# A decoder layer on one core: the norm's factor applied after the products, first up products of block one alone, and the last split moved forward

## The chip, the cores and the metric

The kernel runs on one core of one Trainium2 chip. The metric is the device time of one execution in microseconds (us); it is given as a median of several runs. One of the executions is recorded by the hardware profiler, and all rows of the trace are from that execution. TensorE is called PE, its weight load PEld, VectorE DVE, ScalarE ACT, GpSimd POOL, SyncE (which issues most of the loads) SP.

## The reference

One decoder layer on 256 tokens with 2048 channels, in float32. `rmsnorm(x, g)` is `x * rsqrt(mean(x * x) + 1e-6) * g`.

```
h = rmsnorm(x, norm_mix_pre)
xr, yr, q, k, v, g_rnn, g_attn = split(h @ w_in)
y_rnn = rg_lru(conv(xr)) * gelu(yr)
y_att = attention(rope(q), rope(k), v)          # 32 heads, 4 key heads, window 128, sinks
mix = sigmoid(g_rnn) * (y_rnn @ w_rnn_proj) + sigmoid(g_attn) * (y_att @ w_attn_proj)
x = x + rmsnorm(mix @ w_out, norm_mix_post)
h = rmsnorm(x, norm_mlp_pre)
x = x + rmsnorm(square(relu(h @ w_mlp_up)) @ w_mlp_down, norm_mlp_post)
```

## The kernel before

**Data and weights.** The 256 tokens are two blocks of 128 (`tb` 0 and 1, "block one" and "block two"). Weights come as 128x2048 chunks; class `Stream` (L52) loads each as two half chunks of 128x1024 (512 KB) on SP's queue, in one fixed order, as far ahead as its buffers allow. To keep float32 accuracy with the faster fp32r products, every operand is cut in two parts: `two_parts` (L89) casts the half chunk to `whi` on ACT (L92) and subtracts to get `wlo` on DVE (L93). A product of activations a and weights w is the sum of three matmuls: a high by w high, a low by w high, a high by w low. `split_to`, `ahead` and `half` (L78, L120, L124) make the parts ahead of their use; `split_sums` (L96) does the same for the chunks of the down product that go through a seven-product scheme (`SEVEN`).

**Front.** x is normed before it is transposed: four squares a block (two on ACT L354, two on DVE L358), the norm factor (`rms`, L330), then a multiply by factor and gain (`scale`, L363), where the gain has been spread over the partitions by PE (`gain_b`, L348). `turn` transposes four 128x128 tiles into one bank of PSUM, and `part` cuts them into the high part (ACT, L375) and the low part (DVE, L376) of hT. The first product, keys and values (`kv`), runs between: hi products L390 and L391, lo products L388. For a stretch of this stage the low parts of the weights are made on POOL (`ws.low`, L409). All is pinned in the order written (`keep_in_program_order`). Seven dummy matmuls (L342) stand ahead.

**What follows.** Attention gates and queries by key head group (`b_pass512`, L263), the attention, the recurrent branch (`a_pair`, L225, gives two row blocks of xr or yr; `conv`, `gelu`), the gated merge, and the output product o in two halves of 1024 columns (`b_pass1024`, L854).

**Middle.** `finish` (L888) runs at high priority after each block of o: squares on ACT (L893), multiply by the gains on DVE (L894), `rms`, four multiply-adds L907 that make h2, and `transpose_split` (L277) of four quarters, each one bank with ACT's high part (L285) and DVE's low part (L286) of h2T. Behind block two's norm stand six dummies (L903). Then the up product runs in pairs: `a_pair` takes both blocks at once (hi: 128x512 with the high and the low part of both blocks, L235; lo: 128x256, L238), eight of each in a half chunk. The residual sum (L945, L946) is fed in piece by piece by `pump`.

**Tail.** `down` (L995) is called for each half of the hidden channels and of the columns. In its last call, `early` (L1091) adds the stored first half to four sums on DVE, and `finish` (L1103) takes the four results in turn: DVE adds (L1108), ACT squares (L1112), DVE multiplies by the gain (L1113, L1118), `rms`, four multiply-adds (L1124), and the stores. Instructions of different parts are ordered by a scheduler that follows priorities (`high_priority`), explicit "issue after" edges and pinned sequences.

## Time and profile before

| | us |
|---|---|
| median of 3 runs (lowest, highest) | 1553.24 (1552.12, 1554.74) |
| the profiled execution | 1548.21 |
| its span | 1546.4 |
| PE busy | 1516.1 |
| DVE busy | 1098.4 |
| ACT busy | 824.0 |
| POOL busy | 12.1 |
| mean HBM rate (GB/s) | 192 |

Times in rows of the trace count from the start of the span. A row of the timeline gives start, busy time, engine, line, operation, output and inputs, shape and count; in brackets stands how long the engine was idle ahead of it and what ended that. A row of a group gives busy time in all, mean ns of one, and idle time before it. A matmul's row shows 0.39 us for 128x512, but matmuls are pipelined: the distance from one start to the next is what a matmul costs.

### The profile page before, as it was taken

Reading aid. Unit: us, or ns where it says so; the run is one execution under the profiler, and the core shown is the slowest. Engines: PE = TensorE matmul, PEld = TensorE weight load, DVE = VectorE, ACT = ScalarE, POOL = GpSimd, SP = SyncE. Lnnn points to the kernel's source line nnn. Section 1 sums busy time; section 2 is a strip of 40 time slices with the busy share of each in tenths; the row PEclk is TensorE's granted clock in tenths of the full one; section 3 lists DMA queues with packets and bytes.
Section 4 is the critical chain, followed back from the end, with each engine's and each line's share of the span. In section 5 each row is a group of like instructions: output and inputs, shape, how many; then the busy total and the mean of one; then the engine's idle time right before and its main releaser. Section 6 shows DMA issues by size and latency. Waiting matters only on the chain.

```text
span 1546.4 us, 19944 instructions
## 1 busy us (share of the span) xinstructions
PE 1516.1 (98%) x7562; PEld 1264.5 (82%) x7562; DVE 1098.4 (71%) x1338; ACT 824.0 (53%) x1116; POOL 12.1 (1%) x14
## 2 busy tenths in 40 slices
PE   7999999999999999999999999999999999999996
PEld 5887777788888888888877888888888888888885
DVE  5666666856759867546666876688886766678897
ACT  4545555646647757444354655555454555555552
POOL 3000000000000000000000000000000000000000
PEclk9999999999999999999999999999999999999999
DMA  6454354354655575665663865556667655576663
GB/s 247 161 179 146 127 174 155 125 185 156 227 193 175 166 222 177 203 196 184 243 237 108 271 202 185 190 182 210 215 205 234 204 188 190 181 282 193 202 212 129
DMA packets 82322, 296.19 MB, mean 192 GB/s; under 512 B 9521, under 2 KB 9777, under 8 KB 81201
## 3 DMA queue, kind: packets, MB, share of 16 engines
q1 hardware_dynamic: 78768, 285.48, 56.6%
q10 hardware_dynamic: 3458, 9.45, 1.6%
q8 instruction: 59, 0.97, 0.2%
q14 instruction: 37, 0.30, 0.1%
HBM read 288.60 MB, written 6.29 MB: 191 GB/s over the span
## 4 chain that ended last, share of the span: by engine, by line
PE 81%; DVE 8%; DMA 5%; ACT 3%; issue 2%; DVEq 0%; POOL 0%; ACTq 0%; SPq 0%; POOLq 0%
PE ps L235 21%; PE ps L238 10%; PE dQ L987 5%; DMA wraw<-in_w_dn 4%; DVE wlo L93 4%; PE dP L987 2%; PE s L987 2%; PE gr L253 2%; PE pa L253 2%; PE pr L257 2%; PE pr L255 2%; PE gr L255 2%; PE q L253 2%; PE pr L253 2%; PE gr L257 2%
## 5 line engine op out<-in xcount | busy, mean ns | idle before, releaser
L93 DVE TENSOR_TENSOR wlo<-wraw,whi 128x1024 fp32r<-128x1024 f32 x524 | 635.3, 1222 | 317.5 <-ACT whi L92 316.4
L92 ACT CAST whi<-wraw 128x1024 fp32r<-128x1024 f32 x528 | 549.3, 1050 | 582.5 <-PE ps L235 140.2
L235 PE MATMUL ps<-h2T,whi 128*128 128x512 f32 x1024 | 256.6, 392 | 0.6 <-DVE h2T L286 0.6
L235 PEld LDWEIGHTS ps<-h2T,whi 128*128 128x128 f32 x1024 | 184.2, 189 | 33.8 <-DVE h2T L286 0.8
L238 PEld LDWEIGHTS ps<-h2T,wlo 128*128 128x128 f32 x1024 | 139.7, 190 | 10.0
L238 PE MATMUL ps<-h2T,wlo 128*128 128x256 f32 x1024 | 142.8, 282 | 0.0
L235 PE MATMUL ps<-hT,whi 128*128 128x512 f32 x512 | 130.2, 394 | 0.0
L987 PE MATMUL dQ<-whi,uT 128*128 128x512 f32 x288 | 106.9, 390 | 0.0
L235 PEld LDWEIGHTS ps<-hT,whi 128*128 128x128 f32 x512 | 91.7, 189 | 18.0 <-issue 1.8
L238 PEld LDWEIGHTS ps<-hT,wlo 128*128 128x128 f32 x512 | 70.0, 190 | 5.0
L238 PE MATMUL ps<-hT,wlo 128*128 128x256 f32 x512 | 71.9, 283 | 0.0
L987 PEld LDWEIGHTS dQ<-whi,uT 128*128 128x128 f32 x288 | 54.2, 188 | 11.3 <-ACT whi L92 0.3
L987 PE MATMUL dQ<-wlo,uT 128*128 128x512 f32 x144 | 56.5, 393 | 4.6 <-DVE wlo L93 4.6
L987 PE MATMUL dCs<-whi,uT 128*128 128x512 f32 x144 | 54.5, 395 | 0.0
L112 DVE TENSOR_TENSOR tlo<-t,thi 128x1536 fp32r<-128x1536 f32 x28 | 49.2, 1756 | 7.3 <-ACT thi L111 7.1
L987 PE MATMUL dP<-whi,uT 128*128 128x512 f32 x144 | 53.8, 389 | 0.0
L253 PE MATMUL ga<-whi,hT 128*128 128x512 f32 x128 | 51.2, 400 | 0.0
L253 PE MATMUL q<-whi,hT 128*128 128x512 f32 x128 | 51.1, 399 | 0.0
L257 PE MATMUL ga<-whi,hT 128*128 128x512 f32 x128 | 50.3, 393 | 0.0
L255 PE MATMUL ga<-wlo,hT 128*128 128x512 f32 x128 | 50.3, 393 | 0.0
L255 PE MATMUL q<-wlo,hT 128*128 128x512 f32 x128 | 50.2, 392 | 0.0
L253 PE MATMUL gr<-whi,hT 128*128 128x512 f32 x128 | 50.0, 391 | 0.0
(272 smaller groups left out, 2581.3 us busy)
## 6 DMA issues: line engine op xcount, KB each, us to landing
wraw<-in_w_up SPq DMA_DIRECT2D x128, 512.0 KB, 4.6
wraw<-in_w_dn SPq DMA_DIRECT2D x128, 512.0 KB, 4.6
wraw<-in_w_g SPq DMA_DIRECT2D x64, 512.0 KB, 4.7
wraw<-in_w_xy SPq DMA_DIRECT2D x64, 512.0 KB, 4.5
wraw<-in_w_q SPq DMA_DIRECT2D x32, 512.0 KB, 4.2
wraw<-in_w_ap SPq DMA_DIRECT2D x32, 512.0 KB, 3.8
wraw<-in_w_rp SPq DMA_DIRECT2D x32, 512.0 KB, 4.4
wraw<-in_w_out SPq DMA_DIRECT2D x32, 512.0 KB, 5.0
```

Of the source, the lines that this page charges most:

```text
L92: self.pin(self.nc.scalar.copy(hi, src))
L93: self.pin(self.low.tensor_tensor(lo, src, hi.bitcast(F32), ALU.subtract))
L112: v.tensor_tensor(lo, t, hi.bitcast(F32), ALU.subtract)
L235: mm(both, hi[:, k * P : k * P + P], a.rearrange("p a b -> p (a b)"), start=half == 0 and k == 0, stop=False)
L238: mm(ps[:, f, 1, :], lo[:, k * P : k * P + P], a[:, 0, :], start=False, stop=half == 1 and k == 7)
L253: mm(banks[tb][n], a[:, 0, t], hi[:, n * 512 : n * 512 + 512], start=first, stop=False)
L255: mm(banks[tb][n], a[:, 0, t], lo[:, n * 512 : n * 512 + 512], start=False, stop=False)
L257: mm(banks[tb][n], a[:, 1, t], hi[:, n * 512 : n * 512 + 512], start=False, stop=last)
L987: mm(b, a[x], w[y], start=not begun and i == 0, stop=tail and i == 2)
```

## The change

Four things are joined.

**Front.** x is transposed as it comes. The gain is no longer spread by PE; it is loaded as a 128x16 column table (`gcol`, on ACT's queue) and applied by the copy that takes a tile out of PSUM, tile by tile: `quad` has four 128x128 copies with a scale on ACT, and four multiply-subtracts on DVE; `both` the same with two 128x256. The norm factor r0 comes later: it goes into the rope tables, into the copy of v, into the scale of the tanh of both gates (`rhalf`), and, spread over the partitions by two matmuls (`spread_r`), into a multiply on DVE after each pair of xr and yr (`r_all`, 16 in all). The squares stand behind the kv product. The loads of x and of the first weights alternate by halves. POOL makes no low parts any more.

PE at the start of the program, before (x is the input block, kv the two sums):

```order
L342 MATMUL warm<-ones 128x128 x7
L348 MATMUL gain_b<-gain,ones 128x512 x4
L369 MATMUL ptr<-ident,x_76 128x128 x8
L390 MATMUL kv_141<-whi_169,hT_137 128x512
L391 MATMUL kv_141<-whi_169,hT_137 128x512
L390 MATMUL kv_141<-whi_169,hT_137 128x512
L391 MATMUL kv_141<-whi_169,hT_137 128x512
L369 MATMUL ptr<-ident,x_76 128x128 x4
L390 MATMUL kv_141<-whi_175,hT_137 128x512
L391 MATMUL kv_141<-whi_175,hT_137 128x512
L390 MATMUL kv_141<-whi_175,hT_137 128x512
```

and after the change (front is a PSUM bank that takes four transposed tiles, hT their two parts):

```order
L366 MATMUL warm<-ones 128x128 x7
L387 MATMUL front<-ident,x_76 128x128 x8
L366 MATMUL warm<-ones 128x128 x4
L429 MATMUL kv_126<-whi_153,hT_120 128x512 x4
L387 MATMUL front<-ident,x_77 128x128 x8
L436 MATMUL kv_126<-wlo_155,hT_120 128x512 x2
L429 MATMUL kv_127<-whi_153,hT_120 128x512 x4
L429 MATMUL kv_126<-whi_189,hT_120 128x512 x4
L436 MATMUL kv_127<-wlo_155,hT_120 128x512 x2
L436 MATMUL kv_126<-wlo_191,hT_120 128x512 x2
L429 MATMUL kv_127<-whi_189,hT_120 128x512 x4
```

Gone are the four gain products between the dummies and the first transposes; four more dummies stand behind the first eight transposes, and block two's first transposes come behind four kv products, where they came behind twelve and all of block one's transposes.

**Middle.** The dummies of block two's norm go. The high parts of the first six half chunks of up are made during the end of o (`high_to`; four of them in two spare rooms, `uphi`), together with two whole splits. Their hi products are cut by block: `ahead_of` runs those of block one right behind o, while block two's norm goes on, then block two's, with block two's transposes at fixed places between; the low products of both blocks follow, six half chunks in a row. Two of o's banks are copied to SBUF on ACT so that they come free.

DVE at the end of o, before (h_6164 is block one, h_6165 block two; h2T_6174 to 6177 are the four quarters of the MLP's input):

```order
L907 SCALAR_TENSOR_TENSOR h_6164<-h_6164,st,xg_6162 128x512 x4
L286 TENSOR_TENSOR h2T_6174<-ptr,h2T_6174 128x4x128
L894 TENSOR_TENSOR h_6165<-o_6503,gpg_6157 128x512
L286 TENSOR_TENSOR h2T_6175<-ptr,h2T_6175 128x4x128
L286 TENSOR_TENSOR h2T_6176<-ptr,h2T_6176 128x4x128
L894 TENSOR_TENSOR h_6165<-o_6504,gpg_6157 128x512
L334 TENSOR_REDUCE st<-sqs 128x1
L336 RECIPROCAL st<-st 128x1
L907 SCALAR_TENSOR_TENSOR h_6165<-h_6165,st,xg_6163 128x512 x2
L286 TENSOR_TENSOR h2T_6177<-ptr,h2T_6177 128x4x128
L907 SCALAR_TENSOR_TENSOR h_6165<-h_6165,st,xg_6163 128x512 x2
L286 TENSOR_TENSOR h2T_6174<-ptr,h2T_6174 128x4x128
```

and after the change (h_6211 is block one, h_6212 block two, h2T_6221 to 6224 the quarters):

```order
L951 SCALAR_TENSOR_TENSOR h_6211<-h_6211,st,xg_6209 128x512 x4
L305 TENSOR_TENSOR h2T_6221<-ptr,h2T_6221 128x4x128
L943 TENSOR_TENSOR h_6212<-o_6550,gpg_6204 128x512
L305 TENSOR_TENSOR h2T_6222<-ptr,h2T_6222 128x4x128
L943 TENSOR_TENSOR h_6212<-o_6551,gpg_6204 128x512
L356 TENSOR_REDUCE st<-sqs 128x1
L305 TENSOR_TENSOR h2T_6223<-ptr,h2T_6223 128x4x128
L358 RECIPROCAL st<-st 128x1
L951 SCALAR_TENSOR_TENSOR h_6212<-h_6212,st,xg_6210 128x512 x4
L305 TENSOR_TENSOR h2T_6224<-ptr,h2T_6224 128x4x128
L305 TENSOR_TENSOR h2T_6221<-ptr,h2T_6221 128x4x128
L305 TENSOR_TENSOR h2T_6222<-ptr,h2T_6222 128x4x128
```

The last low part of block one (h2T_6224, before h2T_6177) stood between block two's multiply-adds, and now stands behind all four; the first part of block two follows it at once.

**Tail.** In the last call of `down` the last half chunk is split as soon as the last of the seven-product chunks is through; the sums of `early` and the gain multiplies on the stored half are told to issue behind that split.

DVE in the tail before (wlo_12544 and wlo_12548 are the low parts of the last chunk's two halves):

```order
L93 TENSOR_TENSOR wlo_12544<-wraw_12469,whi_12543 128x1024
L1029 TENSOR_TENSOR t<-s_12047,t 128x512
L1118 TENSOR_TENSOR acc_11400<-acc_11400,g_12539 128x512
L1030 TENSOR_TENSOR t<-s_12048,t 128x512
L1094 TENSOR_TENSOR t<-t,acc_11401 128x512
L1031 TENSOR_TENSOR t<-t,s_12048 128x512
L1032 TENSOR_TENSOR t<-t,s_12048 128x512
L1094 TENSOR_TENSOR t<-t,acc_11400 128x512
L1094 TENSOR_TENSOR t<-t,acc_11401 128x512
L1094 TENSOR_TENSOR t<-t,acc_11400 128x512
L93 TENSOR_TENSOR wlo_12548<-wraw_12471,whi_12547 128x1024
L1118 TENSOR_TENSOR acc_11400<-acc_11400,g_12539 128x512
```

and after the change (wlo_12617 and wlo_12621):

```order
L106 TENSOR_TENSOR wlo_12617<-wraw_12558,whi_12615 128x1024
L106 TENSOR_TENSOR wlo_12621<-wraw_12560,whi_12619 128x1024
L1128 TENSOR_TENSOR t<-s_12136,t 128x512
L1129 TENSOR_TENSOR t<-s_12137,t 128x512
L1201 TENSOR_TENSOR t<-t,acc_11490 128x512
L1130 TENSOR_TENSOR t<-t,s_12137 128x512
L1131 TENSOR_TENSOR t<-t,s_12137 128x512
L1201 TENSOR_TENSOR t<-t,acc_11489 128x512
L1201 TENSOR_TENSOR t<-t,acc_11490 128x512
L1201 TENSOR_TENSOR t<-t,acc_11489 128x512
L1217 TENSOR_TENSOR acc_11489<-dQ_12140,t 128x512
L1228 TENSOR_TENSOR acc_11489<-acc_11489,g_12636 128x512
```

The second low part stood behind nine other operations and now follows the first directly; these operations, but for one gain multiply that goes further back, stand behind it.

The core of the diff:

```diff
+    def high_to(self, n):
+        for j in range(self.split, n):
+            self.load_to(j + 1)
+            self.highs[j] = self.high(self.raw[j], j)
+    def high(self, src, j):
+        hi = self.high_rooms.pop(j, None)
+        if hi is None:
+            hi = self.pool.tile([P, 1024], F32R, tag="whi", bufs=WHALF, name=f"whi{j}")
+        self.pin(self.nc.scalar.copy(hi, src))
+        return hi
     def two_parts(self, src, j):
-        hi = self.pool.tile([P, 1024], F32R, tag="whi", bufs=WHALF, name=f"whi{j}")
+        hi = self.highs.pop(j) if j in self.highs else self.high(src, j)
         lo = self.pool.tile([P, 1024], F32R, tag="wlo", bufs=WHALF, name=f"wlo{j}")
-        self.pin(self.nc.scalar.copy(hi, src))
-        self.pin(self.low.tensor_tensor(lo, src, hi.bitcast(F32), ALU.subtract))
+        self.last_low = self.pin(self.nc.vector.tensor_tensor(lo, src, hi.bitcast(F32), ALU.subtract))
...
+    gcol = const.tile([P, KT], F32, name="gcol")
+    pin(nc.scalar.dma_start(gcol, g_cols))
+    def load_x(tb, half):
+        c = slice(half * 1024, half * 1024 + 1024)
+        return pin(nc.sync.dma_start(x_nat[tb][:, c], x_v[tb][:, c]))
+    ws.pin_load = pin
+    load_x(0, 0)
+    ws.load_to(1)
+    load_x(1, 0)
+    ws.load_to(4)
+    load_x(0, 1)
+    last = load_x(1, 1)
+    ws.load_to(2 * EXTRA + WRAW)
...
+    def quad(tb, q, low):
+        t = slice(tb * P, tb * P + P)
         for i in range(4):
             k = 4 * q + i
-            pin(nc.tensor.transpose(ps[:, i * P : i * P + P], x_nat[tb][:, k * P : k * P + P], ident))
-    def part(tb, q):
-        t = slice(tb * P, tb * P + P)
-        p3 = ps_t.pop((tb, q)).rearrange("p (a b) -> p a b", a=4)
-        hi = hT[q][:, :, 0, t]
-        pin(nc.scalar.copy(hi, p3))
-        pin(nc.vector.tensor_tensor(hT[q][:, :, 1, t], p3, hi.bitcast(F32), ALU.subtract))
+            src = xT[tb, q][:, i * P : i * P + P]
+            if low:
+                pin(nc.vector.scalar_tensor_tensor(act(k, 1, t), src, gcol[:, k : k + 1], act(k, 0, t).bitcast(F32),
+                                                   ALU.mult, ALU.subtract))
+            else:
+                pin(nc.scalar.activation(act(k, 0, t), src, AF.Copy, scale=gcol[:, k : k + 1]))
+    def both(j, low):
+        for i in range(2):
+            k = 2 * j + i
+            src = xT[j][:, i * S : i * S + S]
+            if low:
+                pin(nc.vector.scalar_tensor_tensor(act(k, 1), src, gcol[:, k : k + 1], act(k, 0).bitcast(F32),
+                                                   ALU.mult, ALU.subtract))
+            else:
+                pin(nc.scalar.activation(act(k, 0), src, AF.Copy, scale=gcol[:, k : k + 1]))
...
+    dummies(WARM)
+    for q in range(2):
+        turn((0, q), bank(psm, "front"), [(0, 4 * q + i) for i in range(4)])
+    dummies(WARM_ON)
+    quad(0, 0, False)
     split(1)
-    part(0, 1)
+    quad(0, 0, True)
+    square(0, 0, True)
+    kv_hi(0, 0)
+    for q in range(2):
+        turn((1, q), front_bank(q), [(1, 4 * q + i) for i in range(4)])
+    kv_lo(0, 0)
+    quad(1, 0, False)
+    quad(1, 0, True)
+    kv_hi(0, 1)
     split(2)
-    kv_part(0, 0, False)
-    turn(0, 2)
-    scale(0, 3, r)
-    square(1, 0)
-    square_v(1, 1)
-    square(1, 2)
-    square_v(1, 3)
-    kv_part(1, 0, False)
-    turn(0, 3)
-    kv_part(0, 0, True)
-    r = rms(1, 0)
-    scale(1, 0, r)
-    part(0, 2)
-    turn(1, 0)
+    kv_hi(1, 0)
+    kv_lo(0, 1)
+    kv_lo(1, 0)
+    kv_hi(1, 1)
+    kv_lo(1, 1)
+    for tb in range(TB):
+        quad(tb, 1, False)
     split(3)
-    scale(1, 1, r)
-    part(0, 3)
-    kv_part(1, 0, True)
-    turn(1, 1)
-    kv_part(2, 0, False)
-    part(1, 0)
+    for tb in range(TB):
+        quad(tb, 1, True)
+    for tb in range(TB):
+        kv_hi(2, tb)
     split(4)
-    part(1, 1)
-    kv_all(0, 1)
-    scale(1, 2, r)
-    turn(1, 2)
-    kv_part(2, 0, True)
-    kv_part(3, 0, False)
-    kv_all(1, 1)
-    ws.low = nc.vector
-    part(1, 2)
-    scale(1, 3, r)
-    turn(1, 3)
-    split(5)
-    kv_part(3, 0, True)
-    part(1, 3)
-    kv_all(2, 1)
-    kv_all(3, 1)
-    split(6)
+    for tb in range(TB):
+        kv_lo(2, tb)
+    for j in (4, 5):
+        turn(j, front_bank(j - 2), [(tb, 2 * j + i) for i in range(2) for tb in range(TB)])
+    for tb in range(TB):
+        kv_hi(3, tb)
+    for tb in range(TB):
+        kv_lo(3, tb)
+    for j in (6, 7):
+        turn(j, bank(psm, "front"), [(tb, 2 * j + i) for i in range(2) for tb in range(TB)])
     for j in range(4, 8):
-        if j == 4:
-            ws.pin = lambda i: i
-        if j > 5:
-            held.append(ws.half())
+        both(j, False)
+        split(j + 1)
+        both(j, True)
         for tb in range(TB):
-            kv_all(j, tb)
+            kv_hi(j, tb)
+        for tb in range(TB):
+            kv_lo(j, tb)
+    ws.pin = lambda i: i
+    ws.ahead(7)
...
+        for t in (cc, ss):
+            nc.vector.tensor_scalar(t[:, tb], t[:, tb], r0[tb], None, ALU.mult)
+    rhalf = small("rhalf", [P, TB])
+    for tb in range(TB):
+        nc.vector.tensor_scalar(rhalf[:, tb : tb + 1], r0[tb], 0.5, None, ALU.mult)
+    r_all = small("r_all", [P, S])
+    def spread_r():
+        pr = bank(psm, "pr")
+        for tb in range(TB):
+            dg = t2("dg")[:, 0:P]
+            nc.vector.tensor_scalar(dg, ident, r0[tb], None, ALU.mult)
+            mm(pr[:, tb * P : tb * P + P], ones, dg, start=True, stop=True)
+        nc.scalar.copy(r_all, pr[:, 0:S])
...
+        nc.vector.tensor_tensor(p3, p3, r_all.unsqueeze(1).to_broadcast([P, 2, S]), ALU.mult)
...
+        if name == "o1":
+            for i in range(OPEN_ROOMS // 2):
+                room = flat(unit("uphi"))
+                for k in range(2):
+                    ws.high_rooms[ws.at + 2 * i + k] = room[:, k * 1024 : k * 1024 + 1024]
+            ws.split_to(ws.at + 2)
+            ws.high_to(ws.at + OPEN)
...
-                warm = pair("warm")[:, 0, 0, 0:P]
-                for i in range(WARM_NORM):
-                    mm(warm, ones, junk[:, 0:P], start=True, stop=True)
...
+                for i in range(2):
+                    nc.scalar.copy(og[:, tb, quarter(2 + i)], banks[i])
+                    late.append((tb, 2 + i, og[:, tb, quarter(2 + i)]))
+                return
...
+    def ahead_of(tb, block, half):
+        t = slice(tb * P, tb * P + P)
+        hi = parts[2 * block + half][0]
+        dst = front[block // 2][:, block % 2, :, t]
+        for k in range(8):
+            kt = half * 8 + k
+            fix(mm(dst, hi[:, k * P : k * P + P], h2T[kt // 4][:, kt % 4, :, t], start=tb == 0 and kt == 0, stop=False))
+    def turn_one(q):
+        with tc.high_priority(PRIO):
+            transpose_split(h2[1], h2T, 1, q, turned[q % 2], fix)
+    for half in range(2):
+        ahead_of(0, 0, half)
+    for half in range(2):
+        ahead_of(0, 1, half)
+    turn_one(0)
+    turn_one(1)
+    for half in range(2):
+        ahead_of(0, 2, half)
+    ahead_of(1, 0, 0)
+    turn_one(2)
+    turn_one(3)
+    ahead_of(1, 1, 0)
+    ahead_of(1, 2, 0)
+    for block in range(3):
+        ahead_of(1, block, 1)
...
+    with tc.issue_after(order[1, AFTER][0]), tc.issue_after(order[1, AFTER][1]):
+        parts = [ws.half(False) for j in range(OPEN)]
+    u_first = u2("u")
+    for block in range(3):
+        for half in range(2):
+            lo = parts[2 * block + half][1]
+            for k in range(8):
+                kt = half * 8 + k
+                fix(mm(front[block // 2][:, block % 2, 1, :], lo[:, k * P : k * P + P], h2T[kt // 4][:, kt % 4, 0, :],
+                       start=False, stop=kt == KT - 1))
+            if block == 0 and half == 0:
+                ws.ahead(ws.at - 1)
+            pump()
+        if block == 1:
+            a_sum(front[0], wide(u_first), PRIO)
...
+                    if f == 1 and n == 1:
+                        ws.split_to(2 * len(chunks))
...
+            with tc.issue_after(ws.last_low.ins) if n == 1 else ExitStack():
+                for (tb, i), t in ready.items():
+                    c = quarter(2 * n + i)
+                    behind = nc.vector.tensor_tensor(t, t, acc[tb][:, c], ALU.add)
+                    if n == 1:
+                        ws.last_low = behind
...
+                with tc.issue_after(ws.last_low.ins):
+                    for k in range(2):
+                        c = quarter(k)
+                        nc.vector.tensor_tensor(acc[tb][:, c], acc[tb][:, c], g3[0][:, c], ALU.mult)
```

More of the change, by code (lines that the diff above doesn't have):

```diff
@@ L337, in rms @@
         return a
-    warm = bank(psb, "warm")
-    for i in range(WARM):
-        mm(warm[:, 0:P], ones, ones, start=True, stop=True)
-    gain_b = []
-    for q in range(4):
-        if q % 2 == 0:
-            room = pair("gain_b")
-        gain_b.append(room[:, q % 2].rearrange("p a b -> p (a b)"))
-        mm(gain_b[q], ones, gain[:, quarter(q)], start=True, stop=True)
-    hT = units("hT")
-    pin = ws.pin = tc.keep_in_program_order
-    ps_t = {}
-    def square(tb, q):
-        pin(nc.scalar.activation(t2("j"), x_nat[tb][:, quarter(q)], AF.Square, accum_out=sq[:, 0, tb, q : q + 1]))
@@ L356, in square_v @@
[L356 to L366 removed]
+    warm = bank(psm, "warm")
@@ new lines, in dummies, with front_bank, square @@
+    def dummies(n):
+        for i in range(n):
+            pin(mm(warm[:, 0:P], ones, ones, start=True, stop=True))
+    hT = units("hT")
+    wide_banks = [pair("front") for i in range(2)]
+    def front_bank(i):
+        return wide_banks[i % 2][:, i // 2].rearrange("p a b -> p (a b)")
+    xT = {}
+    def square(tb, q, v=False):
+        c = quarter(q)
+        if v:
+            pin(nc.vector.scalar_tensor_tensor(t2("j"), x_nat[tb][:, c], 1.0, x_nat[tb][:, c], ALU.mult, ALU.mult,
+                                               accum_out=sq[:, 0, tb, q : q + 1]))
+        else:
+            pin(nc.scalar.activation(t2("j"), x_nat[tb][:, c], AF.Square, accum_out=sq[:, 0, tb, q : q + 1]))
@@ L367, in turn, with act @@
+    def turn(key, ps, tiles):
+        xT[key] = ps
+        for i, (tb, k) in enumerate(tiles):
+            pin(nc.tensor.transpose(ps[:, i * P : i * P + P], x_nat[tb][:, k * P : k * P + P], ident))
+    def act(k, part, t=slice(0, S)):
+        return hT[k // 4][:, k % 4, part, t]
+    def quad(tb, q, low):
+        t = slice(tb * P, tb * P + P)
         for i in range(4):
             k = 4 * q + i
-            pin(nc.tensor.transpose(ps[:, i * P : i * P + P], x_nat[tb][:, k * P : k * P + P], ident))
@@ L456, in layer, with kv_hi, kv_lo @@
-    kv_all(3, 1)
-    split(6)
+    def kv_hi(j, tb, parts=(0, 1)):
+        t = slice(tb * P, tb * P + P)
+        for part in parts:
+            for i in range(2):
+                kt = 2 * j + i
+                pin(mm(kv[tb][0], act(kt, part, t), held[j][0][:, quarter(i)], start=kt == 0 and part == 0,
+                       stop=False))
+    def kv_lo(j, tb):
+        t = slice(tb * P, tb * P + P)
+        for i in range(2):
+            kt = 2 * j + i
+            pin(mm(kv[tb][0], act(kt, 0, t), held[j][1][:, quarter(i)], start=False, stop=kt == KT - 1))
@@ L466, in layer @@
+    r0 = [rms(tb, 0) for tb in range(TB)]
     pos_i = pa.tile([P, TB], I32, name="pos_i")
@@ L532, in keys_values @@
         for tb in range(TB):
-            nc.scalar.copy(v_sb[:, tb, :], banks[tb][:, 256:512])
+            nc.scalar.activation(v_sb[:, tb, :], banks[tb][:, 256:512], AF.Copy, scale=r0[tb])
             k2 = t2("k2")
@@ L696, in gelu @@
         a_pair(hT, wide(py))
+        nc.vector.tensor_tensor(wide(py), wide(py), r_all.unsqueeze(1).to_broadcast([P, 2, S]), ALU.mult)
         u = t2("u")
@@ L868, in b_pass1024 @@
             finish(tb, banks[tb])
-        if name == "o1":
-            with tc.issue_after(order[1, AFTER][0]), tc.issue_after(order[1, AFTER][1]):
-                ws.ahead(ws.at - 1)
-        else:
+        if name != "o1":
             ws.ahead(ws.at - 1)
@@ L928, in layer @@
             finish_late()
+    fix = tc.keep_in_program_order
+    parts = [(ws.highs.get(ws.at + j), None) if ws.at + j in ws.highs else ws.parts[ws.at + j] for j in range(OPEN)]
+    front = [pair("ps") for i in range(2)]
+    turned = [bank(psb, "ptr") for i in range(2)]
+    def ahead_of(tb, block, half):
+        t = slice(tb * P, tb * P + P)
+        hi = parts[2 * block + half][0]
[21 more added lines that the diff above has]
+        ahead_of(1, block, 1)
     diag = []
@@ L1055, in layer @@
         for p in range(PAIRS):
-            u = u2("u")
-            a_pair(h2T, wide(u), PRIO if p == PAIRS - 1 else 0)
+            if f == 0 and p == 0:
+                u = u_first
+            else:
+                u = u2("u")
+                prio = PRIO if p == PAIRS - 1 or f == 0 and p == 1 else 0
+                if f == 0 and p == 1:
+                    a_pair(h2T, wide(u), prio, front[1], (1,))
+                else:
+                    a_pair(h2T, wide(u), prio)
             full.append((p, u))
```

104 lines of the change are left out of this document (34 added, 70 removed).

## The prediction

> **What bounds the kernel now.** I read the busy shares first, then TensorE's (PE's) waits, then short windows around the waits.
>
> ```profile
> PE 1516.1 (98%) x7562; PEld 1264.5 (82%) x7562; DVE 1098.4 (71%) x1338; ACT 824.0 (53%) x1116; POOL 12.1 (1%) x14
> ```
>
> PE is busy for 1516.1 of 1546.4 us. The change keeps nearly all matrix products, so it can win from three places only: PE's idle 30 us, time in which PE works at half clock, and the drain behind the last product. PE's waits, by engine and line (total, times, longest):
>
> ```profile
> PE dQ L987 <- DVE wlo L93: 4.6, 2, 4.3
> PE gain_b L348 <- DMA gain<-in_gains: 4.1, 1, 4.1
> PE ptr L369 <- DVE hT L376: 2.0, 1, 2.0
> PE kv L388 <- POOL wlo L93: 1.7, 1, 1.7
> PE ptr L282 <- DVE h L907: 1.5, 2, 1.2
> PE kv L390 <- ACT whi L92: 1.2, 1, 1.2
> ```
>
> Four rows lie in the front (9.0 us), one in the middle, one in the tail. Windows around them, with PE, PEld, DVE, ACT, POOL busy, then the granted clock:
>
> ```profile
> 13.20:16.60 3.40, 2.22 (x12) 1.22 (x11) 1.98 (x3) 1.60 (x3) 0.00 (x0) 1.00 1.03 413
> 20.03:23.44 3.41, 0.83 (x3) 0.30 (x2) 2.91 (x5) 0.81 (x3) 1.74 (x1) 1.00 1.03 414
> 23.44:26.86 3.42, 2.30 (x8) 2.02 (x9) 2.85 (x5) 2.53 (x4) 2.37 (x1) 0.50 0.96 356
> 26.86:30.27 3.41, 3.41 (x12) 2.72 (x11) 1.50 (x3) 0.97 (x2) 2.37 (x1) 0.50 0.03 8
> 460.00:500.00 40.00, 40.00 (x241) 35.63 (x241) 34.67 (x49) 30.50 (x47) 0.00 (x0) 1.00 0.54 176
> 835.81:839.23 3.42, 1.94 (x17) 1.54 (x15) 3.31 (x6) 1.21 (x3) 0.00 (x0) 1.00 0.02 5
> 842.20:859.10 16.90, 16.90 (x97) 14.87 (x98) 15.08 (x17) 10.57 (x16) 0.00 (x0) 1.00 0.81 252
> 1521.90:1525.31 3.41, 0.00 (x0) 0.00 (x0) 3.41 (x6) 0.00 (x0) 0.00 (x0) 1.00 0.00 0
> 1525.31:1528.73 3.42, 3.39 (x8) 2.72 (x9) 3.06 (x5) 0.72 (x2) 0.00 (x0) 0.50 0.00 0
> ```
>
> The waits cost twice. A stretch with 0.83 of 3.41 us busy, and one with none, are each followed by half clock (0.50). A stretch 65% busy (2.22 of 3.40) and one 57% busy (1.94 of 3.42) are not. The half clock lasts until a stretch is fully busy: 6.8 us in the front, 3.4 in the tail.
>
> **Front.** The end of the first product (kv) is the first matmul of the next one:
>
> ```profile
> 4.93 0.63 ACT L354 ACTIVATE j<-x 128x512 f32<-128x512 f32 x1 [2.70 <-DMA x<-in_x]
> 6.16 0.63 ACT L354 ACTIVATE j<-x 128x512 f32<-128x512 f32 x1 [0.50 <-DMA x<-in_x]
> ```
> ```profile
> 8.54 5.12 PE L348 MATMUL gain_b<-gain,ones 128*128 128x512 f32 x6 [4.10 <-DMA gain<-in_gains]
> 14.36 1.04 PE L369 MATMUL ptr<-ident,x 128*128 128x128 f32 x8
> 24.56 1.12 PE L369 MATMUL ptr<-ident,x 128*128 128x128 f32 x4 [2.00 <-DVE hT L376]
> 48.24 0.39 PE L253 MATMUL ga<-whi,hT 128*128 128x512 f32 x1
> 48.46 0.39 PE L255 MATMUL ga<-wlo,hT 128*128 128x512 f32 x1
> ```
> ```profile
> L92 ACT CAST whi<-wraw 128x1024 fp32r<-128x1024 f32 x528 | 549.3, 1050 | 582.5 <-PE ps L235 140.2
> L93 DVE TENSOR_TENSOR wlo<-wraw,whi 128x1024 fp32r<-128x1024 f32 x524 | 635.3, 1222 | 317.5 <-ACT whi L92 316.4
> L533 ACT COPY v_sb<-kv 128x256 f32<-128x256 f32 x2 | 0.7, 368 | 0.8 <-PE kv L388 0.8
> L597 ACT ACTIVATE s<-s,stat 128x128 f32<-128x128 f32 x32 | 12.4, 390 | 1.1 <-DVE stat L591 1.1
> L978 DVE TENSOR_TENSOR e<-e,u 128x128 f32<-128x128 f32 x14 | 4.0, 285 | 0.0
> ```
>
> The loads land at 4.9, 6.1 and, by this spacing, every 1.25 us after. Removed are the broadcast of the gain (PE waits for it until 8.54 and works on it until 14.4), the norm ahead of the transposes, the eight gain multiplies, and POOL's part in the splits (DVE and ACT do them all). The rows give these unit costs: matmul 128x512 0.22 us from start to start (48.24, 48.46), a transpose 0.11 (eight in 1.04), twice that at half clock; a split 1.05 on ACT and 1.22 on DVE; a scaled 128x128 copy on ACT 0.27 (between nothing and L597's 0.39, by the slope to L533's 0.37), a 128x128 DVE operation 0.2 to 0.285.
>
> Now the chain. Transposes of block one's first tiles 4.9 to 6.0 (half clock); four scaled copies to 7.3; whi0 to 8.4; wlo0 to 9.6, because on DVE it stands ahead of the four low parts; these end at 10.3. The second group of transposes takes the same bank, so PE waits here for about 4 us, until 10.3. Then its transposes, four dummies and four kv products at half clock, to about 14.5; block two's transposes; four copies and low parts behind them, about 16.6; PE works on from there with small waits (whi2 on ACT behind eight copies and whi1, about 19.9), until low part four is ready, about 21.5. From there PE is the bound: 70 of the 96 kv products x 0.227 = 15.9, 16 transposes x 0.11 = 1.8. End 39.2 against 48.24, a gain of 9.0. The two fp32 products that spread the norm factor cost back 0.4 to 0.5: **-8.5 us**.
>
> The landing of the gain column (128 small rows) appears in no row. Its ends: with the first load (4.9, gains 0.3 us), or as late as the old gain row, 8.5 (loses 2.4 us). I take the second load's 6.1, the nearest in kind and time. Front: -6 to -11.
>
> **Factor applied later.** Sixteen multiplies with r_all, each like the evacuation's 0.68 us, sum to 11 us on DVE, spread over the stage of xr and yr with the attention's output product and the recurrence's gates between. Of the 40 us windows that I read there, 460 to 500 is the densest: DVE is busy for 34.67, and PE never waits. Two or three multiplies add 2 us. I count them at nothing; without that cover they would cost up to 11. The scaled tanh and copies replace unscaled ones.
>
> **Middle.** DVE's rows around the end of the last product before the MLP, then PE's:
>
> ```profile
> 836.08 1.42 DVE L907 SCALAR_TENSOR_TENSOR h<-h,st,xg 128x512 f32<-128x512 f32 x2
> 838.01 1.41 DVE L907 SCALAR_TENSOR_TENSOR h<-h,st,xg 128x512 f32<-128x512 f32 x2
> ```
> ```profile
> 834.67 0.71 PE L903 MATMUL warm<-j,ones 128*128 128x128 f32 x4 [0.83 <-ACT j L893]
> 842.14 1.20 PE L235 MATMUL ps<-h2T,whi 128*128 128x512 f32 x4 [0.60 <-DVE h2T L286]
> 859.01 1.32 PE L235 MATMUL ps<-h2T,whi 128*128 128x512 f32 x5
> ```
>
> Between 833.84 and 842.14 PE does dummies and transposes; then six half chunks take 16.9 us, to 859.01. The change starts block one's products at once, but the work ahead of them on ACT grows: two copies of o (128x512, about half a cast each) and two casts (1.05 each). I carry that as 0.6 us of delay to the end of o (834.4) and 1.1 to block one's chain. The first product then waits for low part two, 835.3; the transposes of part four go at 836.75. Low part four stands on DVE behind block two's four multiply-adds (four at 0.67, 836.1 to 839.4 before); with 0.7 us for itself it is ready at about 840.3. PE idles for some 2.5 us there. Behind it everything is dense: 80 of 96 hi products of 128x256 x 0.12 = 9.6, eight transposes 0.9, 48 low products x 0.12 = 5.8, some small waits of block two's parts (about 1.5): 858.1. So **-0.9 us**. The split of 48 wide products (0.227) into 96 half ones (0.12) adds 0.6 in it. Without the wait for low part four it would be about -3.4; with both of the doubtful delays doubled, +1.
>
> **Tail.** DVE, then PE and ACT:
>
> ```profile
> 1516.46 1.22 DVE L93 TENSOR_TENSOR wlo<-wraw,whi 128x1024 fp32r<-128x1024 f32 x1 [1.94 <-ACT whi L92]
> 1522.26 1.89 DVE L1094 TENSOR_TENSOR t<-t,acc 128x512 f32<-128x512 f32 x3
> 1524.06 1.22 DVE L93 TENSOR_TENSOR wlo<-wraw,whi 128x1024 fp32r<-128x1024 f32 x1
> 1537.67 0.69 DVE L1108 TENSOR_TENSOR acc<-dQ,t 128x512 f32<-128x512 f32 x1 [1.91 <-PE dQ L987]
> 1539.93 1.41 DVE L1124 SCALAR_TENSOR_TENSOR x<-acc,st,x 128x512 f32<-128x512 f32 x2
> ```
> ```profile
> 1525.34 0.79 PE L987 MATMUL dQ<-wlo,uT 128*128 128x512 f32 x1 [4.27 <-DVE wlo L93]
> ```
> ```profile
> 1517.19 1.05 ACT L92 CAST whi<-wraw 128x1024 fp32r<-128x1024 f32 x1 [0.28 <-DMA wraw<-in_w_dn]
> ```
>
> The last low part moves ahead of nine DVE operations. Its high part ends at 1518.2, so it runs to 1519.5; PE still waits about 0.9 us (its own data are late now), not 4.27, and the half clock goes (1.7). PE would end 5 us earlier, at about 1532. But the operations stand behind it, each 0.60 from start to start (three in 1.89), and DVE then has no idle time: eight to 1524.2, five to 1527.2, three and the norm step to 1529.9, four multiply-adds to 1532.5, dP's and dQ's pairs, the second norm step, and the last multiply-adds start at 1536.1 instead of 1539.93. DVE, not PE, sets the end: **-3.9 us**. If PE set it, -5; if the operations behind wlo cost 0.68 each and not 0.60, -2.5.
>
> **Sum.** -8.5 - 0.9 - 3.9 = -13.3 us. The profiled execution took 1548.2 (span 1546.4 and 1.8 around it); the median of the runs is 1553.24, 5.0 above it. I take the difference over: 1553.24 - 13.3 = **1540 us** (profiled: 1534.9).
>
> **Rivals.**
> - *Half clock in the middle.* Between 836.9 and 840.3 PE would be busy 0.8 us. If a stretch lies there as 20.03:23.44 lay in the front, half clock follows for one stretch: +1.7, 1541.6. Against it: a stretch placed otherwise holds 47 to 59% of work, and 57% did no harm. [...]
> - *A late front.* The gain column lands at 8.5, or the clock stays at half until about 24 because of the thinner start: +2.4 to +5, 1542.5 to 1545.
> - *No wait in the middle, or a quicker start:* -2.5 to -3, 1537.
> - *The r_all multiplies are not covered:* up to +11, 1551, within measurement of no change. For it only DVE's 34.67 of 40; against it PE's 40.00.
> - *Slower.* The front's bursts never fill a stretch, so all of kv runs at half clock: 25.3 us of work (96 x 0.227 + 32 x 0.11) becomes 50.6 behind 13 us, end 64 against 48: +15 there, -4.8 elsewhere, 1563. It decides if no stretch before 39 is full; 13 to 21 us holds about 7.5 of 8.5, so I hardly believe it.
>
> **How the numbers follow.** Forecast 45%; half clock 20%; late front 14%; quicker 13%; multiplies 5%; slower 3%. The range reaches from the quicker case with some of the front's better end (1535) to the late front with the clock drop (1546). A measurement here tells 0.2%, 3.1 us, from no change. Faster 0.92, same 0.05, slower 0.03.
>
> **What would show it.** In the new profile: the first matmul of ga at 39 to 40; a wait of front transposes for the low parts of hT near 4 us; a wait of ps for h2T near 2.5 us; the wait for the last wlo near 0.9 us; DVE without idle time from 1505 on the new scale. A first ga after 42, PE waits in the gates of xr and yr, or PE as the releaser of the last DVE chain would show a step wrong.

## The result, and the profile after

| | before | after |
|---|---|---|
| median of 6 runs, us | 1552.23 (1551.27 to 1554.74) | 1542.89 (1541.20 to 1547.62) |
| ratio | | 0.9942, 95% interval 0.9926 to 0.9958 |
| the profiled execution, its span | 1548.21, 1546.4 | 1543.42, 1541.6 |

The change takes 9.3 us off the median (interval of the ratio: 6.5 to 11.5 us). Forecast were 13.3 us, and 1540 in a range of 1535 to 1546. The two profiled executions differ by only 4.8 us; the execution of before which was profiled is the odd one. With 1548.21 us it lies below every timed run of before on record (the lowest is 1549.12).

PE's waits in the profile of the change (total, times, longest):

```profile
PE front L387 <- DVE hT L399: 4.5, 1, 4.5
PE dQ L1084 <- DVE wlo L106: 3.6, 4, 1.4
PE ps L990 <- DVE h2T L305: 3.2, 2, 2.3
PE ptr L301 <- DVE h L951: 1.4, 1, 1.4
PE ps L251 <- DVE u L262: 1.1, 1, 1.1
PE dQ L1084 <- ACT whi L100: 0.9, 1, 0.9
```

The waits for the gain, for POOL's low parts and the one 4.3 us wait in the tail are gone. In their place stand the wait of the second group of transposes (4.5 us) and that for the fourth low part of block one (2.3), both forecast, and several of about 1 us in the down product and at the third pair of the up product, which were not.

PE's timeline in the front, the middle and the tail of the change:

```profile
10.53 1.11 PE L387 MATMUL front<-ident,x 128*128 128x128 f32 x4 [4.46 <-DVE hT L399]
13.01 2.06 PE L429 MATMUL kv<-whi,hT 128*128 128x512 f32 x4
14.86 1.67 PE L387 MATMUL front<-ident,x 128*128 128x128 f32 x8
22.61 1.79 PE L429 MATMUL kv<-whi,hT 128*128 128x512 f32 x6 [0.64 <-DVE hT L399]
40.55 0.39 PE L272 MATMUL ga<-whi,hT 128*128 128x512 f32 x1
...
828.02 1.22 PE L990 MATMUL ps<-h2T,whi 128*128 128x256 f32 x8 [0.93 <-DVE h2T L305]
832.73 2.65 PE L990 MATMUL ps<-h2T,uphi 128*128 128x256 f32 x20 [2.31 <-DVE h2T L305]
850.68 2.00 PE L251 MATMUL ps<-h2T,whi 128*128 128x512 f32 x8
857.51 2.11 PE L251 MATMUL ps<-h2T,whi 128*128 128x512 f32 x8 [1.08 <-DVE u L262]
...
1515.20 0.50 PE L1084 MATMUL dQ<-whi,uT 128*128 128x512 f32 x1 [0.88 <-ACT whi L100]
1516.46 0.51 PE L1084 MATMUL dQ<-wlo,uT 128*128 128x512 f32 x1 [0.76 <-DVE wlo L106]
1518.39 0.80 PE L1084 MATMUL dQ<-wlo,uT 128*128 128x512 f32 x1 [0.76 <-DVE wlo L106]
```

The front's steps come within half a microsecond of the forecast chain up to 14.9 us, and 1.1 late from 22.6 on. In the tail the last split is no longer alone: the last two half chunks of the weights both come late. PE waits 0.88 us for the high part and 0.76 for the low part of the one, and 0.76 for the low part of the other. Windows (PE, PEld, DVE, ACT, POOL busy, granted clock):

```profile
828.52:831.93 3.41, 1.86 (x15) 1.45 (x13) 3.37 (x8) 0.88 (x2) 0.00 (x0) 1.00 0.02 5
1514.60:1518.01 3.41, 1.68 (x4) 0.67 (x4) 2.12 (x2) 2.08 (x3) 0.00 (x0) 1.00 0.92 312
1518.01:1521.43 3.42, 3.04 (x7) 2.47 (x8) 3.31 (x6) 0.00 (x0) 0.00 (x0) 0.50 0.01 2
```

A stretch with 1.68 of 3.41 us busy is followed by half clock (tail), one with 1.86 is not (middle). The forecast had the tail's half clock gone; it stays, and the three short waits lie in or across the ends of the stretch ahead of it (1514.60 to 1518.01).

To follow where time goes, this table gives the start of the same PE instruction in each trace, less its start in the first trace of before (there at 48.24, 742.36, 1021.47, 1366.22 and 1514.27 us, and the last end at 1537.63). "Last two down" is a product 0.7 us behind the start of the last but one of the four calls of `down`; from there on only the last two calls run. "Chunk 14" is the first product with the 14th of the last call's 16 chunks, where the last three chunks begin; between these two columns lie 148 us in before. (The expectations call this stretch the last down product, and count to its last chunk, where the change has lost 5.5 us and not 3.9.)

| trace | first ga | first o | first down | last two down | chunk 14 | PE's end | median us (runs) | less before, us |
|---|---|---|---|---|---|---|---|---|
| after | -7.7 | -6.6 | -7.0 | -6.7 | -2.8 | -4.8 | 1542.89 (6) | -9.3 |
| after_again | -7.7 | -6.6 | -5.9 | -5.8 | -1.4 | -2.5 | 1542.58 (6) | -11.1 |
| before_again | 0.7 | 0.7 | 2.0 | 2.3 | 5.5 | 6.8 | 1555.15 (1) | |
| undo_front | 0.6 | 0.5 | 4.9 | 4.9 | 7.8 | 6.1 | 1548.95 (12) | -4.8 |
| undo_middle | -8.0 | -6.9 | -7.4 | -6.3 | -3.2 | -4.8 | 1544.10 (5) | -9.6 |
| undo_tail | -8.3 | -7.1 | -5.4 | -6.1 | -3.1 | -2.8 | 1548.92 (6) | -4.8 |
| front_bank | -13.0 | -11.9 | -11.3 | -11.4 | -6.7 | -9.0 | 1541.22 (6) | -10.4 |
| mid_order | -8.2 | -7.1 | -5.6 | -5.7 | -2.2 | -5.8 | 1543.35 (6) | -8.3 |
| spread_reload | -8.8 | -7.7 | -9.7 | -9.4 | -5.7 | -11.4 | 1540.43 (5) | -11.2 |
| bank_and_reload | -12.8 | -11.7 | -12.2 | -12.9 | -10.7 | -16.2 | 1535.00 (4) | -16.7 |
| before_reload | -1.1 | -1.2 | 0.3 | 0.4 | 1.8 | 1.7 | 1549.73 (12) | -2.0 |
| no_r_all | -7.4 | -6.9 | -7.2 | -7.3 | -3.7 | -5.6 | 1542.74 (1) | |

The last column compares with the median of before in the same comparison: 1552.23 for after, 1553.71 for after_again and the three with a part undone, 1551.66 for the next three, 1551.70 for bank_and_reload and before_reload.

### The profile page after: what moved, and what is told of

Same layout as the page of the kernel before. It is cut to its first block, busy times and chain, and to the rows that moved or that the text cites. A ratio compares the mean times of both kernels' runs of the same rounds, so it can differ in the third digit from the quotient of the medians.

```text
span 1541.6 us, 20059 instructions
## 1 busy us (share of the span) xinstructions
PE 1513.7 (98%) x7602; PEld 1266.1 (82%) x7602; DVE 1105.1 (72%) x1373; ACT 827.6 (54%) x1133; POOL 1.7 (0%) x9
## 4 chain that ended last, share of the span: by engine, by line
PE 80%; DVE 8%; DMA 7%; ACT 3%; issue 2%; SPq 0%; DVEq 0%; ACTq 0%
PE ps L251 20%; PE ps L254 10%; DMA wraw<-in_w_dn 5%; PE dQ L1084 4%; DVE wlo L106 3%; PE s L1084 2%; PE dP L1084 2%; PE gr L272 2%; PE pa L272 2%; PE gr L274 2%; PE pr L272 2%; PE pr L274 2%; PE pr L276 2%; PE pa L274 2%; PE q L272 2%
## 5 line engine op out<-in xcount | busy, mean ns | idle before, releaser
L251 PE MATMUL ps<-h2T,whi 128*128 128x512 f32 x976 | 244.6, 393 | 1.1 <-DVE u L262 1.1
L251 PEld LDWEIGHTS ps<-h2T,whi 128*128 128x128 f32 x976 | 175.7, 189 | 32.6 <-DVE u L262 1.3
L254 PEld LDWEIGHTS ps<-h2T,wlo 128*128 128x128 f32 x976 | 133.2, 191 | 9.5
L254 PE MATMUL ps<-h2T,wlo 128*128 128x256 f32 x976 | 136.2, 283 | 0.0
L1084 PEld LDWEIGHTS dQ<-whi,uT 128*128 128x128 f32 x288 | 54.2, 188 | 12.8 <-ACT whi L100 1.7
L272 PE MATMUL pr<-whi,yrnn 128*128 128x512 f32 x128 | 50.1, 391 | 0.0
```

The source lines that it names most:

```text
L251: mm(both, hi[:, k * P : k * P + P], a.rearrange("p a b -> p (a b)"), start=half == 0 and k == 0, stop=False)
L254: mm(ps[:, f, 1, :], lo[:, k * P : k * P + P], a[:, 0, :], start=False, stop=half == 1 and k == 7)
L272: mm(banks[tb][n], a[:, 0, t], hi[:, n * 512 : n * 512 + 512], start=first, stop=False)
L1084: mm(b, a[x], w[y], start=not begun and i == 0, stop=tail and i == 2)
```

## The experiments

**Undoing one part of the change each.** In undo_front everything of the first section of the change is as before; in undo_middle the up product begins as before, with the dummies; in undo_tail these lines go:

```diff
-                    if f == 1 and n == 1:
-                        ws.split_to(2 * len(chunks))
...
-            with tc.issue_after(ws.last_low.ins) if n == 1 else ExitStack():
...
-                with tc.issue_after(ws.last_low.ins):
```

> The change with the front of before (gain and norm factor ahead of the transposes, no later multiplies). My theory: the three parts add up, and the front is worth the 7.4 us by which the first query product starts earlier in the trace of the change (63.74 against 71.10). So this kernel keeps 9 - 7.4 = about 2 to 4 us against before, some 1548 to 1550, and its trace starts that product at 71.1 and the tail's last split behind the first. Rival: the weight stream in the last down product, not PE's start, sets the end; then an earlier front is given back there and this kernel is as fast as the change, 9 us under before.

> The change with the middle of before (no products of block one alone, six dummies back). My theory: the middle gives 0.3 to 1.6 us only, since PE waits 2.3 us for the fourth low part of block one and 1.1 us for a bank of the third pair; so this kernel is within 1.5 us of the change. Rival: the middle costs as much as it gives (0), or it is what gives 3 us or more and the rest is noise.

> The change with the tail of before (last split behind nine DVE operations). My theory: the tail gives 3.5 us at the same arrival of the last weights, so this kernel is 3 to 4 us slower than the change, its last dQ wait for wlo near 4 us again. Second point: the trace of the change loses 5.5 us against before between the start of the last down product and its last chunk (waits for wlo of 0.7 and 1.4 us, then 1.6 us for late data). If that loss came with the moved split it is gone here; if it is the load stream's delay behind the four 1 MB reloads at 1365 us, it is here too, or comes and goes between runs of one kernel.

> The change itself once more, for its spread and a second trace. If the loss of 5.5 us in the last down product comes from the landing times of loads, its size differs from the first trace by more than 1 us while the front (first ga at 40.55) and the middle repeat within 0.2 us. If it is fixed by the order of instructions, the waits there repeat as well (0.74 and 1.38 us).

The ratios to before are 0.9976 (0.9965 to 0.9987), 0.9937 (0.9924 to 0.9950), 0.9969 (0.9956 to 0.9981), and 0.9934 (0.9923 to 0.9945) for the change itself. So the front is worth 6.4 us by the medians, the tail 6.3, the middle 1.5; the intervals of the first two lie apart from that of the change itself, the middle's does not. (Each is known to about 2.5 us, and together they give 14.2, where the whole change has 11.1.) The front fits the 6.7 us that its traces still hold at the first o. (The rest of undo_front's row says little: its profiled execution was the slowest of its twelve, 1554.32 us.) For the tail the traces say less than the median: between chunk 14 and PE's end undo_tail goes from -3.1 to -2.8, the change from -2.8 to -4.8 and in its second trace from -1.4 to -2.5. That makes 2.3 and 1.4 us, against an interval that reaches from about 3 to 8 us. The profiled execution of undo_tail was the fastest of its six (1545.48 us, median 1548.92), so its trace is not the typical one; how the 6.3 us come about is not shown. The last split's own wait is visible in undo_tail, but with 1.05 us it is far below the expected 4, since the weights are late there as well:

```profile
1515.97 0.79 PE L1084 MATMUL dQ<-whi,uT 128*128 128x512 f32 x1 [1.65 <-ACT whi L100]
1517.22 0.79 PE L1084 MATMUL dQ<-wlo,uT 128*128 128x512 f32 x1 [0.47 <-DVE wlo L106]
1524.10 0.50 PE L1084 MATMUL dQ<-wlo,uT 128*128 128x512 f32 x1 [1.05 <-DVE wlo L106]
```

Two further things follow. All these traces give back 2.9 to 4.4 us between the start of the last two down products and chunk 14, where the instructions are those of before; undo_tail does too, so the loss does not belong to the moved split. In after_again it is 4.4 us, with waits for wlo of 0.77 and 0.83 in place of 0.74 and 1.38; by the 1 us that was set beforehand this does not tell landing times from the order of instructions. And after_again shows the rival of the half clock in the middle, which the first trace of the change does not. Its windows:

```profile
828.95:832.36 3.41, 1.09 (x9) 0.89 (x8) 3.18 (x5) 0.59 (x1) 0.00 (x0) 1.00 0.00 0
832.36:835.78 3.42, 3.42 (x17) 3.42 (x18) 0.00 (x0) 0.00 (x0) 0.00 (x0) 0.50 0.00 0
```

The same wait of 2.3 us lies here in one stretch with only 1.09 us of work, and the clock halves; the first down product then starts at -5.9 where the first trace has -7.0. In the first trace the end of a stretch, at 831.93, cuts the wait in two; the stretches on both sides have 1.86 and 2.62 us of work, and the clock is 1.00 in both. undo_front and undo_tail lose it as well, behind stretches with 1.09 us of work each: in undo_tail the clock is 0.57 over 833 to 837 us, and in undo_front the 20 products behind the wait take 4.16 us, where the first trace of the change has 2.65.

**Before once more.** The kernel is that of before.

> The kernel before once more, for a second trace. The five traces of kernels with the change's weight stream, and those with one part undone, lose 3.5 to 5.9 us between the start of the last down product and its last chunk, measured against the one trace of before; the instructions there are the same. Theory: that one trace of before was a lucky one, and this one loses 3 to 6 us there too, with waits of dQ for wlo of 0.5 to 1.5 us and a span of 1549 to 1552. Rival: before loses nothing there again (span within 1 us of 1546.4), and the change makes the late weights.

Its span is 1553.3, above the 1549 to 1552 expected, and it goes from 2.3 to 5.5 us in the stage in question. In the view of PE's waits the row of dQ has grown from two waits to four:

```profile
PE dQ L987 <- DVE wlo L93: 5.9, 4, 4.1
```

So the loss occurs in both kernels, and the trace from which the forecast was made was a lucky one. This second one is the other extreme: with 1555.15 us it is the slowest execution of before on record. (Of the other differences 1.3 us come in before's own middle, where the clock is 0.50 from 840.16 to 843.57, and 0.7 in the front.)

**The front's bank.** The dummies write into a bank that is used last, so that the second group of transposes has one of its own:

```diff
-    warm = bank(psm, "warm")
...
+    warm = front_bank(3)
```

> The change with the dummies in another bank, so that the second group of transposes does not wait for the first one's low parts. My theory: the 4.5 us wait goes, the kv products start at about 8.5 to 10.5 instead of 13.0, and kv ends 2 to 3 us earlier (first ga at 37.5 to 38.5; 40.55 in the change), if the clock is up by then; the time falls by 2 to 3 us. Rival: the next wait takes its place (whi1 and whi2 behind the copies on ACT, or the loads of x and of the first weights), and ga starts within 0.7 us of 40.55.

```profile
4.99 1.12 PE L387 MATMUL front<-ident,x 128*128 128x128 f32 x8 [0.56 <-DMA x<-in_x]
5.95 1.06 PE L372 MATMUL front<-ones 128*128 128x128 f32 x8
7.84 0.73 PE L429 MATMUL kv<-whi,hT 128*128 128x512 f32 x2 [0.83 <-ACT whi L100]
9.37 0.76 PE L429 MATMUL kv<-whi,hT 128*128 128x512 f32 x2 [0.79 <-DVE hT L399]
```

The wait goes and kv starts at 7.84. The first ga stands at 35.24, 5.3 us earlier than in the change, twice what was expected: between 5 and 16 us PE waits 0.83 us at most at a time, and from 12.18 on six products of kv take 1.73 us; in the change, at half clock from 9.3 to 16.2 (0.50), four take 2.06. But the median does not follow: it stands 10.4 us below before (ratio 0.9931, 0.9917 to 0.9946), where the change stands 9.3 and 11.1 below. The trace holds -11.4 at the start of the last two down products, and only -6.7 at chunk 14.

**The order in the middle.** Three of block two's multiply-adds wait for the fourth low part:

```diff
+                with tc.issue_after(order[0, 3][1]) if tb == 1 and q > 0 else ExitStack():
                     nc.vector.scalar_tensor_tensor(h2[tb][:, c], h2[tb][:, c], r1[tb], xg[tb][:, c], ALU.mult, ALU.add)
```

> The change with three of block two's four multiply-adds told to issue behind the fourth low part of block one. My theory: the wait of ps for h2T falls from 2.3 us to about 0.9, the half clock that follows it in two of three traces goes, and the down product starts 1.4 us earlier against o than in the change (1.4 to 3 with the clock). Rival: block two's norm is now later and its transposes or the weights' low parts wait instead: no change.

Of the waits of that trace, these two belong to the middle:

```profile
PE ps L991 <- DVE h2T L305: 1.9, 2, 0.9
PE o L274 <- DVE wlo L106: 1.7, 2, 0.9
```

The wait fell as expected (longest 0.9), the three windows from 824.9 to 835.1 have 2.39 to 2.46 of 3.40 us busy, and the clock is 1.00 in all of them. The time does not move (ratio 0.9934, 0.9917 to 0.9951). In this trace o itself waits 1.7 us for low parts and 0.9 for a high part, and the first down product starts at -5.6: what is gained behind o is lost in it. That late weights cancel the gain is what this one trace shows, not more.

**The reloads.** At the start of the last but one down product, four transfers of 1 MB bring back the stored sums and the residual. In spread_reload they come in eight pieces, one behind a split:

```diff
-            nc.scalar.dma_start(acc[tb], acc_away[tb])
-            nc.scalar.dma_start(x1[tb], x1_away[tb])
...
+        def reload(p):
+            if p < 8:
+                a, w, tb, i = pieces[p]
+                c = slice(i * 1024, i * 1024 + 1024)
+                with tc.issue_after(ws.last_high.ins):
+                    nc.scalar.dma_start(a[tb][:, c], w[tb][:, c])
```

> The change with the four 1 MB reloads (stored sums and residual) cut in eight and issued one by one behind splits of the last but one down product, instead of all at once at about 1365 us. Theory: the reloads push the load stream back by some 2 us there, with four buffers it never catches up, and the last down product pays 5 us; spread out, the loss from its start to the last chunk falls from 5.5 to 2 us or less, and the time by 2 to 4 us. Rival: the stream is late for another reason (its own rate, the seven-product splits on DVE) and nothing changes.

> The change with both mends, the dummies in another bank and the reloads in eight pieces. Theory: the front is 5 us shorter than in the change, and the last down product gives less of it back than the 2.4 us by which front_bank's gain shrank between the start of that product and the end; so 13 to 15 us under before, 3 to 5 under the change. Rival: the late weights take the front's gain whatever is mended, and it stays at the 10 to 11 us of the single mends.

> The kernel before with the reloads in eight pieces. If the loss in the last down product is a property of both kernels, this alone takes 1 to 4 us off before (its second trace lost 3.9 us there). Rival: only the change suffers from it, and before gains nothing (within 0.7 us).

Two half chunks loaded at that time (numbers 475 and 477) landed 12.4 and 12.7 us after their issue in the change, the second of them 11.0 in before and 12.4 in before_again; in spread_reload 8.2 and 5.8. A window of 15 us over the reloads, in the change and in spread_reload (last columns: clock, DMA share, GB/s):

```profile
1365.00:1380.00 15.00, 15.00 (x68) 12.43 (x67) 9.81 (x11) 5.87 (x6) 0.00 (x0) 1.00 0.98 370
```
```profile
1362.60:1377.60 15.00, 15.00 (x68) 12.41 (x67) 11.63 (x11) 7.36 (x8) 0.00 (x0) 1.00 0.90 318
```

The waits of PE in spread_reload (tlo are the low parts of the sums of weights that the seven-product chunks use, u two row blocks of the up product):

```profile
PE s L1084 <- DVE u L262: 1.8, 2, 1.1
PE dQ L1084 <- DVE tlo L125: 1.6, 2, 1.2
PE dQ L1084 <- DVE wlo L106: 0.6, 2, 0.3
```

In every trace with the four reloads at once, but for the first one of before, PE waits for wlo once or twice between 1430 and 1461 us (0.3 to 1.4 us each), and then for a high part among the last three chunks (0.5 to 1.8). In the three traces with spread reloads neither wait is there. From chunk 14 to PE's end spread_reload and bank_and_reload gain 5.7 and 5.5 us, where the traces with the moved split and the reloads at once gain 1.1 to 3.6; the mean clock of their traces is 0.998 and 0.997, where the change has 0.995.

The measured worth: before_reload against before 0.9986 (0.9975 to 0.9997), 2.0 us by the medians; spread_reload 0.9923 (0.9910 to 0.9936), which is not clear of the 0.9934 (0.9923 to 0.9945) of the change itself; both mends together 0.9899 (0.9885 to 0.9914), which is. They give 1535.0 us, 16.7 under before and more than the 13 to 15 expected. That is the fastest kernel of this study, and it also shows that the front's gain of front_bank comes through once the reloads are spread. So the reloads are one cause of the late weights, but not of the whole loss: spread_reload still goes from -9.4 to -5.7 before chunk 14 (2 us or less were expected), bank_and_reload from -12.9 to -10.7. The trace of spread_reload shows where: 1.1 us go at 1360.8 us, where PE waits for u, and 0.6 and 1.3 at two waits for tlo; wlo is down to 0.6 in all, where the change has 3.6. A wait for u of 0.5 us or more is also in five of the traces with the reloads at once. What makes u and tlo late was not tested.

**The late factor.** The two lines with r_all are taken out; the norm factor is then missing in the recurrent branch.

> The change without its sixteen multiplies by r_all (the norm factor is then missing in the recurrent branch: this leaves out part of the computation). Five traces of kernels with the late factor lose 0.64 us between the first xr product and the first attention product, the one with the old front loses nothing. Theory: the multiplies on DVE delay the softmax that PE's transposes wait for, and the loss is gone here (0.2 us or less); ahead of that stage and behind it nothing differs. Rival: the loss stays at 0.64, and it comes from the other order of the attention's pieces (spread_r, rope tables).

Between the first xr product and the first attention product its offset goes from -7.09 to -7.13, in the change from -7.44 to -6.80. All eight traces of kernels with the late factor lose 0.64 to 0.66 us there, and the three traces with the front of before that can be set against the first one lose nothing. So the sixteen multiplies do cost 0.64 us. How is not shown: PE's wait there for the softmax is not longer with them (0.9 us in the change, 1.3 without), and the difference lies in the spacing of the attention's small products between 278 and 308 us.

## Why the prediction was right

**The front** was forecast at -8.5 and is -7.7 at the first ga, -7.4 behind the two spreading products. The chain was right in every link: the wait for the bank (4 us forecast, 4.46), the low parts behind wlo0, the start of dense work at the third weights. Its mis-sized term is the stretch between: PE is at half clock from 9.32 to 16.15, so that block two's eight transposes end at 16.5; four copies take 1.14 us and not 1.08; whi2 ends at 21 and dense work starts at 22.6, forecast 21.5. The gain column was there in time (it landed at 5.05). The first ga stands at 40.55, just outside the 39 to 40 that the forecast named as its sign.

**The late factor** was costed at nothing and costs 0.64 us. Idle time on DVE in windows of 40 us did not show it.

**The middle** was forecast at -0.9. The first six half chunks end at 850.68; before's 859.01 less the 6.75 us that o's end had by then is 852.26, so this gives -1.6. Then the third pair waits 1.08 us for a bank, because the copy that empties it stands on ACT behind a cast whose data are late. Net -0.4 at the first down product in one trace, +0.7 with the half clock in the other; undo_middle, with the middle of before, has -0.5 over the same stretch. So no gain is shown for the middle. The wait for the fourth low part (2.5 forecast, 2.31) and a half clock behind a stretch that lies as 20.03:23.44 did in the front (seen in after_again) were both named.

**The tail** was forecast at -3.9, with its half clock gone and DVE as the bound. DVE is the bound: it has no idle time from 1517.1 on but for the norm's two square roots, and PE's last product ends at 1532.81, just as DVE comes to it (1532.85). From the last chunk's first low product to the end the change gains 3.5 us (-1.3 to -4.8); in its second trace it is 1.6. The half clock stayed (0.50 from 1518.01 to 1521.43): the last two half chunks of the weights came late, and the 3.41 us ahead of it have 1.68 of work. In spread_reload and bank_and_reload, with a mean clock of 0.998 and 0.997 against 0.995 in the change, the same part of the tail gains 4.4 and 4.5, and in mid_order (0.995) it gains 2.7.

**The sum.** For the profiled execution it failed: forecast 1534.9, measured 1543.42. For the median it was right within its range, but 2 to 4 us too good. The weak step is "I take the difference over", from one execution to the median. The working took the weight stream to shift with PE, and in the profiled execution of before PE never waits between the start of the last two down products and chunk 14. In the other traces of kernels with the reloads at once (before_again among them) 2.9 to 4.7 us are lost there. Counted against the profiled execution the change therefore shows -4.8, and not -13.3. Between the medians the loss largely cancels, as far as the one further trace of before can tell, and what the change's first trace shows for the parts adds up: -7.4 + 0.6 - 3.5 and about zero for the middle make -10.3, where the two comparisons give -9.3 and -11.1. That the two kernels both pay the loss was not foreseen, so the fit of the median is luck in this point. The mis-sized terms (front 1.1, late factor 0.6, middle 0.9, tail 0.4) all point the same way; the range held because they are small.

**The rivals.** Half clock in the middle: true in after_again, undo_front and undo_tail, not in the first trace of the change. A late front: neither of its two conditions came, the gain column at 8.5 or half clock until about 24; the front is 1.1 us short by the slower stretch told above. The r_all multiplies: 0.64 of 11 us. A front that never warms up: no, though the clock is at half from 9.32 to 16.15.

Half clock followed on one wait of 2.3 us (after_again, 1.09 of 3.41 us busy), and on three of 0.76 to 0.88 us (the tail of after, 1.68 of 3.41).

## What to carry to other kernels

A single profiled execution is one draw: before its span is used as the base of a sum, ask which stage depends on landing times, and how the timed runs stand to it. Here their median stood 4 to 5 us higher, and a second trace, 6.9 us longer, lost 3.2 of it in that stage. An earlier PE in front of a stage with four load buffers need not bring anything: the further 5.3 us of front_bank did not show in the median until the reloads were spread. Look for what pushes the load stream back (here 4 MB of reloads at once). In the change the second transposed group shares a bank with the first, and PE waits 4.46 us for the low parts that DVE takes out of it; moving a dummy's bank brought the first ga 5.3 us forward.

## What the runs showed of the hardware

From where the trace has the granted clock on (13.20 us in before, 5.91 in after), it changes before PE is done at 23.44, 30.27, 1525.31 and 1528.72 in before, and at 9.32, 16.15, 1518.01 and 1521.43 in after. These points lie 2, 438 and 1 times 3.41 us apart in before, and 2, 440 and 1 times in after.

The table has stretches of that length at full clock, the work of PE in them, and the clock of the stretch behind. For before and after, those with half clock behind are all there are up to PE's last product, and those with full clock behind are the least busy of their kind.

| trace, start of the stretch | PE busy, us of 3.41 | clock behind |
|---|---|---|
| before, 1521.90 | 0.00 | 0.50 |
| after, 5.91 | 0.16 | 0.50 |
| before, 20.03 | 0.83 | 0.50 |
| after_again, 828.95 | 1.09 | 0.50 |
| after, 1531.67 | 1.14 | 0.50 |
| before_again, 836.75 | 1.60 | 0.50 |
| after, 1514.60 | 1.68 | 0.50 |
| after, 828.52 | 1.86 | 1.00 |
| before, 835.81 | 1.94 | 1.00 |

The longest wait does not sort these rows: the stretch with 1.86 us of work has 1.51 us of one wait in it, and the one with 1.68 meets none over 0.88. What decides between the two is not shown. Half clock ended behind a stretch with 3.04 of 3.42 us busy (after, 1518.01), where the prediction has a fully busy one; it went on behind 2.30 (before, 23.44) and 2.21 (after, 9.32). The stretches lie differently against the program in the two traces of the change: the same 2.3 us wait falls into one stretch in after_again (from 828.95) and the clock halves, and in after it is cut at 831.93 and the clock stays at 1.00.
